# Feed-forward stage of a two-layer decoder trunk: 20 instead of 4 of the 22 inner column tiles computed by rows of tokens, in five blocks of 512, and transposed by transfers

## The chip, the cores and the metric

One Trainium2 chip, one of its cores. The metric is the device time in microseconds (us) of one execution of the whole program; three runs of the kernel before gave 1230.99, 1231.00 and 1232.06 us, so the median is 1231.0 us. A profiled execution lies beside them; every duration in this document that has a row is taken from such a profile.

## What is computed

The input is 256 tokens of 1024 numbers in float32. Two layers each apply a feed-forward half step, a token mixer, and a second feed-forward half step, each followed by a layer norm. Four feed-forward stages in all; the change touches only these. Cut to what matters:

```python
D_MODEL = 1024; SEQ = 256; DEPTH = 2; D_FF = 2816

def _swiglu(x, w1, w3, w2):
    return (jax.nn.silu(x @ w1) * (x @ w3)) @ w2

for l in range(DEPTH):
    h = _swiglu(x, ffn_w1[l, 0], ffn_w3[l, 0], ffn_w2[l, 0])
    x = _layernorm(ALPHA * x + 0.5 * h, ln_g[l, 0], ln_b[l, 0])
    h = _mixer(x, ...)
    x = _layernorm(ALPHA * x + h, ln_g[l, 1], ln_b[l, 1])
    h = _swiglu(x, ffn_w1[l, 1], ffn_w3[l, 1], ffn_w2[l, 1])
    x = _layernorm(ALPHA * x + 0.5 * h, ln_g[l, 2], ln_b[l, 2])
```

The inner width of 2816 is 22 column tiles of 128. All products are float32 products made of three: every operand is split into a high part (`hi`, the value rounded to the format that TensorE multiplies) and the rest (`lo`), and a product is hi·hi + lo·hi + hi·lo.

## The kernel before

**Weights.** `stream` (L148) loads 1 MB of weights (128 x 2048 floats) on SyncE's queue (SP) into one of four `raw` buffers and splits it in two pieces of 1024 columns: ScalarE (ACT) copies each piece into a `hi` buffer (L167), and VectorE (DVE) subtracts to get the `lo` buffer (L169). There are eight `hi` and eight `lo` buffers, used in turn, so a piece can only be split when TensorE (PE) has done with the piece eight before it.

**The stage by columns** (`gemm_a2`, L232). For two column tiles j of the inner width, w1 and w3 of both tiles are streamed (2 MB). The weight piece stands in the array and the tokens move: for each of the four weight tiles 8 matmuls of 512 columns (the hi and the lo part of the 256 tokens beside each other, L242) and 8 of 256 columns with the lo weights (L249). The result has the inner columns on the partitions and the tokens in the row, which is the form that the product with w2 wants as its standing operand. ACT copies half of each bank out (L250), DVE adds (L252), ACT applies Silu (L547), DVE multiplies (L548), and `split` (L195, L196) leaves the tile in `hhi` and `hlo`.

**The stage by rows** (`gemm_b2`, L291, and `gemm_first`, L316, for the very first one). For a block of 512 inner columns, four column tiles, the tokens stand in the array (128 at a time) and the weights move: for each of the two halves of the tokens, each of the two matrices and each of the 8 k-tiles, three matmuls of 512 columns (`three`, L227 to L230). That is 96 matmuls a block, in 16 steps of 6 (`rows_b`, L261); the eight weight pieces are all held from the first half of the tokens, which reads each once, to the second half, which reads each once more and then frees it. After each half of the tokens its result (128 tokens x 512 columns) has the tokens on the partitions and must be transposed. `front` (L521) applies Silu (L524) and multiplies (L525); `turned` (L528) calls `transposed` (L173): GpSimd (POOL) copies the two 16-bit halves of the floats apart (two copies, L184), two 16-bit transposing transfers on SP's queue turn them (L188), POOL puts the halves together again (two copies, L192), and ACT and DVE split the result into `hhi` (L536) and `hlo` (L538).

**Order of the work.** A feed-forward stage before is: one block by rows (column tiles 0 to 3), then nine calls of `gemm_a2` for tiles 4 to 21, then the product with w2 in two passes of 512 output columns, each with 22 k-tiles in 11 steps of 12 matmuls per pass; the first pass keeps the last four k-tiles back to the end of the pass (`tail=4`). The order on PE is the order of the code. On the other engines a scheduler sets it, from data and from `behind`, which puts an instruction after a given one. Small pieces of work run beside PE's as generators: `beside(task, delay)`, `beat(w)` and `yield w` count the progress of PE's work in beats, and a task goes on when its beat has come. ACT, DVE, POOL and SP each work their queue strictly in this order, so an instruction that waits holds back all behind it on its engine.

**Other places that the change touches.** `setup` (L372) loads the tokens and small constants on POOL's queue during the first stage. `bc_load` (L402) loads a norm's gain and bias on POOL's queue into the two `bc` buffers; `Norm.turned` (L479) applies them to the tokens 8 beats after the norm. The `planes` tiles (transposition buffers) come from two `val` buffers.

Of the kernel before, what the change touches and what calls it, by code (L numbers as in the profile page):

```python
# [11 lines left out]
F32 = mybir.dt.float32  # L12
# [4 lines left out]
AF = mybir.ActivationFunctionType  # L17
ALU = mybir.AluOpType
AX = mybir.AxisListType

P = 128
D = 1024
# [3 lines left out]
DEPTH = 2  # L26
DFF = 2816
FT = DFF // P
FB = 4
HEADS = 8  # L30
HD = 64
GROUPS = 8
# [2 lines left out]
CH = 2048  # L35
# [16 lines left out]
def trunk(ctx, tc, x, xT, w13a, w13b, w2, wb, wqk, wa, wbr, wo, gateb, sgug, sgub, sguwT, sgubias, lam, diffg,  # L52
          lng, lnb, lngT, lnbT, cosT, sinT, out):
    nc = tc.nc
    V, A, G, PE = nc.vector, nc.scalar, nc.gpsimd, nc.tensor
# [7 lines left out]
    act = ctx.enter_context(tc.tile_pool(name="act", bufs=27))  # L63
    res = ctx.enter_context(tc.tile_pool(name="res", bufs=2))
# [6 lines left out]
    def name(s):  # L71
        serial[0] += 1
        return f"{s}_{serial[0]}"
# [21 lines left out]
    def t512(s, n=2):  # L95
        return tmp.tile([P, 512], F32, tag="main", name=name(s), bufs=n)
# [37 lines left out]
    def beside(task, delay):  # L134
        tasks.append([clock[0] + delay, task])
# [37 lines left out]
    def transposed(src, out, via, first, second):  # L173

        def planes(v):
            return v.bitcast(U16).rearrange("p (w c) -> p w c", w=2)

        def numbers(v):  # L180
            return v.bitcast(U16).rearrange("p (c w) -> p w c", w=2)

        for w in range(2):
            G.tensor_copy(out=planes(out)[:, w], in_=numbers(src)[:, w])  # L184
        yield first
        with behind(loaded[0]):
            for w in range(2):
                nc.sync.dma_start(planes(via)[:, w].rearrange("p (k t) -> p k t", k=4), planes(out)[:, w],  # L188
                                  transpose=True)
        yield second  # L190
        for w in range(2):
            G.tensor_copy(out=numbers(out)[:, w], in_=planes(via)[:, w])  # L192
# [98 lines left out]
    def gemm_b2(srcs, xh, xl, done, norm=None):  # L291

        lent, after = [()] * 4, [(None, None)] * 4
        if norm:
            lent = [(0, 1), (0,), (), ()]
            after[1:3] = (None, norm.ends[0]), (norm.ends[0], norm.ends[0])
        ps = [[bank() for _ in range(2)] for _ in range(NT)]
        got = [[None] * 4 for _ in range(2)]  # L300
        for t in range(NT):
            for c in range(2):
                if norm:
                    norm.ready(t, c)
                    after[3] = [norm.xlo.get((0, 1))] * 2
                for m in range(2):
                    n = 2 * c + m
                    if t == 0:
                        got[m][2 * c : 2 * c + 2] = stream(srcs[m][:, c * CH : (c + 1) * CH], sub=512, lent=lent[n],
                                                           after=after[n])  # L310
                    for i in range(2 * c, 2 * c + 2):
                        rows_b(ps[t][m], t, 2 * i, got[m][i], xh, xl, KT)
            with behind(latest[0] if t == 0 else None):
                done(t, ps[t])
# [40 lines left out]
    b = side_bank()  # L355
# [159 lines left out]
    def ffn(l, f, i, norm, last=False):  # L515
        xh, xl = parts(both)
        h_hi = [act.tile([P, 512], F32R, tag="slot", name=name("hhi")) for _ in range(FT // 2)]
        h_lo = [act.tile([P, 512], F32R, tag="slot", name=name("hlo")) for _ in range(FT // 2)]
        hh, hl = view(h_hi), view(h_lo)

        def front(t, ps):  # L521
            p = act.tile([P, 2, 512], F32, tag="val", name=name("planes"), bufs=2)
            s = p[:, 1]
            A.activation(s, ps[0], AF.Silu)  # L524
            V.tensor_tensor(out=s, in0=s, in1=ps[1], op=ALU.mult)  # L525
            beside(turned(t, s, p), 0)

        def turned(t, s, p):  # L528
            yield from transposed(s, p[:, 0], p[:, 1], 17, 6)
            x = p[:, 0].rearrange("p (k t) -> p k t", k=4)  # L530
            yield 6
            for j in range(2):
                hi, lo = (v[j].rearrange("p (k t) -> p k t", k=2)[:, :, t * P : (t + 1) * P] for v in (h_hi, h_lo))
                f = x[:, 2 * j : 2 * j + 2]
                with behind(silu[0]):
                    A.activation(hi, f, AF.Copy)  # L536
                with behind(added[0]):
                    V.tensor_tensor(out=lo, in0=f, in1=hi.bitcast(F32), op=ALU.subtract)  # L538

        if norm is None:  # L540
            gemm_first([w13b[l, f, 0], w13b[l, f, 1]], front)
        else:
            gemm_b2([w13b[l, f, 0], w13b[l, f, 1]], xh, xl, front, norm=norm)
        for j in range(FB, FT, 2):
            for m, z in gemm_a2([w13a[l, f, j - FB + m] for m in range(2)], both, lambda m: t512("silu")):
                s = z[:, :T]
                silu[0] = A.activation(s, s, AF.Silu).ins  # L547
                V.tensor_tensor(out=s, in0=s, in1=z[:, T:], op=ALU.mult)  # L548
                split(hh(j + m), hl(j + m), s)
                if norm is None and j + m == FB:  # L550
                    beside(setup(s[:, :1]), 0)
        ln = Norm(l, i, 2.0 * ALPHA, 4.0 * EPS, s[:, :1], last)
        gemm_b(w2[l, f, 0], FT, hh, hl, lambda t, p, c, n: ln.part(t, 0, p))

        def done(t, p, c, n):
            ln.part(t, 512 + c, p)
            if c + n == 512:
                ln.finish(t, ((2, 1.5), (2, 1))[t])

        gemm_b(w2[l, f, 1], FT, hh, hl, done, tail=14, last=((0, 256), (256, 256)) if last else ())  # L560
        return ln.close()
# [228 lines left out]
    norm = None  # L790
# [10 lines left out]
def _layout(i):  # L801
    c = np.ascontiguousarray
    L = DEPTH
    f = {k: np.asarray(v) for k, v in i.items()}
    x = f["x"].reshape(T, D)
    o = {"x": x, "xT": c(x.reshape(T, KT, P).transpose(2, 1, 0)).reshape(P, KT * T)}

    def cols(w):

        k, n = w.shape[-2:]  # L810
        w = w.reshape(*w.shape[:-2], k // P, P, n // P, P)
        a = w.ndim
        return w.transpose(*range(a - 4), a - 2, a - 3, a - 4, a - 1)

    def pairs(w):

        w = cols(w)
        lead = w.shape[:-4]
        n = w.shape[-4]
        w = w.reshape(*lead, n // 2, 2, P, KT, P)  # L820
        a = w.ndim
        return c(w.transpose(*range(a - 4), a - 3, a - 4, a - 2, a - 1)).reshape(*lead, n // 2, P, CH)

    def halves(w):

        k, n = w.shape[-2:]
        w = w.reshape(*w.shape[:-2], k // P, P, n // 512, 512)
        a = w.ndim
        w = c(w.transpose(*range(a - 4), a - 2, a - 3, a - 4, a - 1))
        return w.reshape(*w.shape[:-2], (k // P) * 512)  # L830

    nb = FB * P
    w1, w3 = f["ffn_w1"], f["ffn_w3"]
    o["w13a"] = c(np.stack([cols(w1[..., nb:]), cols(w3[..., nb:])], axis=4)).reshape(L, 2, FT - FB, P, CH)
    o["w13b"] = c(np.concatenate([halves(w1[..., :nb]), halves(w3[..., :nb])], axis=2))
    o["w2"] = halves(f["ffn_w2"])
    u, v, q, k, val, ga, gb = (f["w_in"][:, :, s * D : (s + 1) * D] for s in range(7))
    o["wb"] = np.stack([halves(w) for w in (v, val)], axis=1)
    o["wqk"] = np.stack([pairs(w) for w in (q, k)], axis=2)
    o["wa"] = np.stack([pairs(w) for w in (u, ga, gb)], axis=1)  # L840
    o["wbr"] = pairs(f["w_branch"])
    o["wo"] = halves(f["w_out"])
    o["gateb"] = c(f["gate_b"].reshape(L, 2, KT, P).transpose(3, 0, 1, 2))
    o["sgug"], o["sgub"] = f["sgu_ln_g"], f["sgu_ln_b"]
    o["sguwT"] = c(f["sgu_w"].transpose(0, 3, 1, 2)).reshape(L, P, GROUPS * P)
    o["sgubias"] = f["sgu_b"].reshape(L, GROUPS * P)
    o["lam"] = f["lam"]
# [29 lines left out]
```

## Time and profile before

| What | Value |
|---|---|
| median of three runs | 1231.0 us (1230.99 to 1232.06) |
| the profiled execution | 1231.87 us, its span 1230.2 us (first to last instruction) |
| PE, matmuls | busy 1224.3 us (100% of the span), 6639 matmuls |
| DVE, ACT | busy 890.9 us (72%) and 755.3 us (61%) |
| POOL | busy 161.2 us (13%) |
| DMA | 246.09 MB, mean 200 GB/s |
| granted TensorE clock | 0.999 of full speed |

How to read the views: the page gives for each engine its busy time and share of the span. The chain is the work that ended last, followed back from the last instruction; its pieces in order of time are "start, duration, what, how many". The groups of instructions give for each line, engine and operation the tiles, the count, the busy time and the mean duration of one in ns. Matmuls are pipelined, so the mean duration of one (some 390 ns) is not the distance from one to the next; that distance is read from the chain or from a stretch of the windows. The view of a tile lists the instructions that read or write it with shortest, median and longest duration. A timeline row is "start, duration, engine, line, operation, tiles, count" and in brackets the idle time before and what ended it.

### The profile page before, as it was taken

The page shows a single profiled execution, that of the slowest core. Times are in us where ns is not written, and L with a number is a line of the kernel's source. Part 1 is how long each engine was busy: PE and PEld are TensorE (multiplying, and loading weights), DVE is VectorE, ACT ScalarE, POOL GpSimd, SP SyncE. Part 2 cuts the span into 40 slices and gives each one's busy share as a digit, 9 for nine tenths or more (in the row PEclk, how much of TensorE's full clock was granted, in tenths as well). Part 3 has the DMA queues.
Part 4 walks back from the last instruction along what each step waited for, and adds up shares of the span by engine and source line. Part 5 has one row for each costly group of instructions (what it writes and reads, how often), then busy time and mean ns, then how long its engine had stood idle before and what let it go on. Part 6 is the DMA issues. An engine that isn't in the chain of part 4 may idle for free.

```text
span 1230.2 us, 17916 instructions
## 1 busy us (share of the span) xinstructions
PE 1224.3 (100%) x6639; PEld 1057.5 (86%) x6639; DVE 890.9 (72%) x1532; ACT 755.3 (61%) x1388; POOL 161.2 (13%) x248
## 2 busy tenths in 40 slices
PE   9999999999999999999999999999999999999998
PEld 8888888888888888888888888888888888888887
DVE  6767567886787977665677665678867879766753
ACT  7676446678765566664466664466886654766640
POOL 1300000246400021000021000002462000210000
PEclk9999999999999999999999999999999999999999
DMA  9955645655854747547547547556567456566540
GB/s 344 307 205 181 231 171 176 236 176 167 280 201 140 253 151 230 186 170 256 195 156 225 191 160 254 204 180 205 169 193 277 143 185 226 196 198 205 170 173 35
DMA packets 58089, 246.09 MB, mean 200 GB/s; under 512 B 22752, under 2 KB 23824, under 8 KB 31888
## 3 DMA queue, kind: packets, MB, share of 16 engines
q1 hardware_dynamic: 54032, 232.28, 54.7%
q0 software_dynamic: 3536, 12.13, 3.2%
q8 instruction: 52, 0.85, 0.3%
q10 hardware_dynamic: 432, 0.52, 0.2%
q14 instruction: 37, 0.30, 0.1%
HBM read 235.47 MB, written 1.05 MB: 192 GB/s over the span
## 4 chain that ended last, share of the span: by engine, by line
PE 99%; DMA 0%; DVE 0%; ACT 0%; issue 0%; ACTq 0%
PE bank L242 38%; PE bank L230 36%; PE bank L249 20%; PE bank L345 2%; PE sbank L612 1%; PE sbank L496 1%; PE sbank L664 1%; PE sbank L747 1%; PE sbank L662 0%; DMA xraw<-in_xT 0%; PE sbank L649 0%; PE sbank L654 0%; PE sbank L468 0%; DVE xtok L476 0%; ACT whi L195 0%; DVE st L441 0%
## 5 line engine op out<-in xcount | busy, mean ns | idle before, releaser
L169 DVE TENSOR_TENSOR wlo<-raw,whi 128x1024 fp32r<-128x1024 f32 (+1 forms) x442 | 500.4, 1151 | 225.8 <-PE bank L249 118.5
L167 ACT ACTIVATE whi<-raw 128x1024 fp32r<-128x1024 f32 (+1 forms) x442 | 425.2, 979 | 270.0 <-PE bank L230 132.6
L242 PE MATMUL bank<-x,whi 128*128 128x512 f32 x1792 | 422.7, 391 | 0.0
L242 PEld LDWEIGHTS bank<-x,whi 128*128 128x128 f32 x1792 | 331.5, 188 | 66.7
L249 PE MATMUL bank<-x,wlo 128*128 128x256 f32 x1792 | 231.0, 284 | 0.0
L249 PEld LDWEIGHTS bank<-x,wlo 128*128 128x128 f32 x1792 | 225.6, 191 | 5.6
L230 PE MATMUL bank<-whi,hhi 128*128 128x512 f32 (+1 forms) x374 | 141.2, 378 | 0.0
L230 PE MATMUL bank<-wlo,hhi 128*128 128x512 f32 (+1 forms) x374 | 141.0, 377 | 0.0
L230 PE MATMUL bank<-whi,hlo 128*128 128x512 f32 (+1 forms) x374 | 140.9, 377 | 0.0
L250 ACT ACTIVATE r<-bank 128x256 f32<-128x256 f32 x256 | 96.5, 380 | 67.0 <-PE bank L249 66.8
L230 PE MATMUL bank<-whi,x 128*128 128x512 f32 x328 | 105.7, 393 | 0.0
L230 PEld LDWEIGHTS bank<-whi,hlo 128*128 128x128 f32 x374 | 70.4, 188 | 13.0
L230 PEld LDWEIGHTS bank<-wlo,hhi 128*128 128x128 f32 x374 | 70.4, 188 | 12.7
L230 PEld LDWEIGHTS bank<-whi,hhi 128*128 128x128 f32 x374 | 70.4, 188 | 12.7
L230 PEld LDWEIGHTS bank<-whi,x 128*128 128x128 f32 x328 | 61.6, 188 | 12.6
L230 PE MATMUL bank<-wlo,x 128*128 128x512 f32 x164 | 63.9, 390 | 0.0
L405 POOL DMA_DIRECT2D bc<-in_lng x6 | 3.2, 536 | 454.9 <-DVE bc L404 454.9
L588 POOL TENSOR_TENSOR swap<-swap,sin_t 128x512 f32<-128x512 f32 x16 | 26.5, 1655 | 243.2 <-DMA swap<-z 133.3
L502 ACT ACTIVATE xf<-sbank,ln_b,ln_g 128x128 f32<-128x128 f32 x80 | 30.1, 456 | 40.1 <-PE sbank L496 40.1
L252 DVE TENSOR_TENSOR silu<-bank,r 128x256 f32<-128x256 f32 x144 | 54.2, 417 | 0.0
L184 POOL COPY planes<-planes 128x512 uint16<-128x512 uint16 x16 | 26.1, 1659 | 178.9 <-DVE planes L525 178.9
L437 DVE SCALAR_TENSOR_TENSOR xtok<-xtok,bank 128x512 f32<-128x512 f32 (+1 forms) x25 | 16.5, 662 | 42.2 <-PE bank L230 42.2
(183 smaller groups left out, 1324.1 us busy)
## 6 DMA issues: line engine op xcount, KB each, us to landing
raw<-in_w13a SPq DMA_DIRECT2D x72, 1024.0 KB, 5.0
raw<-in_w SPq DMA_DIRECT2D x40, 1024.0 KB, 4.9
raw<-in_wa SPq DMA_DIRECT2D x24, 1024.0 KB, 6.0
raw<-in_wb SPq DMA_DIRECT2D x16, 1024.0 KB, 5.0
raw<-in_wqk SPq DMA_DIRECT2D x16, 1024.0 KB, 5.1
raw<-in_wbr SPq DMA_DIRECT2D x16, 1024.0 KB, 5.2
raw<-in_w13b SPq DMA_DIRECT2D x12, 1024.0 KB, 4.9
raw<-in_wo SPq DMA_DIRECT2D x8, 1024.0 KB, 4.9
```

The source lines that it names most:

```text
L167: A.activation(h, r, AF.Copy)
L169: V.tensor_tensor(out=w, in0=r, in1=h.bitcast(F32), op=ALU.subtract)
L184: G.tensor_copy(out=planes(out)[:, w], in_=numbers(src)[:, w])
L230: PE.matmul(ps, xx, w, start=start and n == 0, stop=stop and n == 2)
L242: PE.matmul(b[-1], hi[:, k * P : (k + 1) * P], xc(k), start=k == 0, stop=False)
L249: PE.matmul(b[n][:, :T], lo[:, k * P : (k + 1) * P], xc(k)[:, :T], start=False, stop=k == KT - 1)
L250: emptied[0] = A.activation(r[:, s], b[n][:, T:], AF.Copy, scale=scale).ins
L252: a = V.tensor_tensor(out=z[:, s], in0=b[n][:, :T], in1=r[:, s], op=ALU.add)
L345: PE.matmul(ps[t][m], x[:, j, o + t * P : o + (t + 1) * P], y, start=k0 + j == 0 and o == 0 and y is hi, stop=k0 + j == KT - 1 and y is lo)
L437: V.scalar_tensor_tensor(out=self.y[t][:, s], in0=self.y[t][:, s], scalar=self.scale, in1=ps, op0=ALU.mult, op1=ALU.add)
L502: A.activation(xf[:, s], b[:, s], AF.Identity, scale=self.gT[:, f], bias=self.bT[:, f])
L588: turned_by[0] = G.tensor_tensor(out=s3, in0=s3, in1=s, op=ALU.mult).ins
```

## The change

Of each feed-forward stage, column tiles 0 to 15 and 18 to 21 are now computed by rows, in five blocks of 512; only tiles 16 and 17 are left to one call of `gemm_a2`, which stands after the fifth block. The fifth block is tiles 18 to 21, the last four k-tiles of the product with w2. The weights are laid out accordingly (`w13a`, `w13b`). `front` and `turned` take the number of the block; the waits ahead of the transfers become 13.3 and 10.3 beats, and those behind them 0.6. The transposition buffers come from `val` for even blocks and from the norm's `bc` buffers for odd ones. Silu and multiplication of a block are now what `behind(silu[0])` and `behind(added[0])` refer to, and `setup` is called after the first half of the tokens of block 1. Since two lines are new near the top, line numbers are two higher up to `ffn` (the matmul of L230 stands on L232) and five to eleven higher behind it.

```diff
-FB = 4
+NB = 5
+FB = 4 * NB
+FA = FB - 4
...
-        def front(t, ps):
-            p = act.tile([P, 2, 512], F32, tag="val", name=name("planes"), bufs=2)
-            s = p[:, 1]
-            A.activation(s, ps[0], AF.Silu)
-            V.tensor_tensor(out=s, in0=s, in1=ps[1], op=ALU.mult)
-            beside(turned(t, s, p), 0)
-
-        def turned(t, s, p):
-            yield from transposed(s, p[:, 0], p[:, 1], 17, 6)
+        def front(n, wait):
+
+            def done(t, ps):
+                pool, tag = ((act, "val"), (res, "bc"))[n % 2]
+                p = pool.tile([P, D], F32, tag=tag, name=name("planes"), bufs=2).rearrange("p (w c) -> p w c", w=2)
+                s = p[:, 1]
+                silu[0] = A.activation(s, ps[0], AF.Silu).ins
+                added[0] = V.tensor_tensor(out=s, in0=s, in1=ps[1], op=ALU.mult).ins
+                beside(turned(n, t, s, p, wait[t]), 0)
+                if norm is None and (n, t) == (1, 0):
+                    beside(setup(s[:, :1]), 0)
+            return done
+
+        def turned(n, t, s, p, wait):
+            yield from transposed(s, p[:, 0], p[:, 1], wait, 0.6)
             x = p[:, 0].rearrange("p (k t) -> p k t", k=4)
-            yield 6
+            yield 0.6
             for j in range(2):
-                hi, lo = (v[j].rearrange("p (k t) -> p k t", k=2)[:, :, t * P : (t + 1) * P] for v in (h_hi, h_lo))
+                k = (n * 4 if n < NB - 1 else FT - 4) // 2 + j
+                hi, lo = (v[k].rearrange("p (k t) -> p k t", k=2)[:, :, t * P : (t + 1) * P] for v in (h_hi, h_lo))
...
-        if norm is None:
-            gemm_first([w13b[l, f, 0], w13b[l, f, 1]], front)
-        else:
-            gemm_b2([w13b[l, f, 0], w13b[l, f, 1]], xh, xl, front, norm=norm)
-        for j in range(FB, FT, 2):
-            for m, z in gemm_a2([w13a[l, f, j - FB + m] for m in range(2)], both, lambda m: t512("silu")):
+        for n in range(NB):
+            srcs = [w13b[l, f, m * NB + n] for m in range(2)]
+            if n == 0 and norm is None:
+                gemm_first(srcs, front(n, (10.3, 10.3)))
+            else:
+                gemm_b2(srcs, xh, xl, front(n, (13.3, 10.3)), norm=norm if n == 0 else None)
+        for j in range(FA, FT - 4, 2):
+            for m, z in gemm_a2([w13a[l, f, j - FA + m] for m in range(2)], both, lambda m: t512("silu")):
                 s = z[:, :T]
                 silu[0] = A.activation(s, s, AF.Silu).ins
                 V.tensor_tensor(out=s, in0=s, in1=z[:, T:], op=ALU.mult)
                 split(hh(j + m), hl(j + m), s)
-                if norm is None and j + m == FB:
-                    beside(setup(s[:, :1]), 0)
```

How the instructions move, at three places of the first stage. On PE, just after the first block (`bank` is an accumulator bank, `x_129` and `x_130` the two halves of the k-tiles of the tokens, `whi` and `wlo` weight pieces), before:

```order
L242 MATMUL bank_403<-x_129,whi_395 128x512 x4
L242 MATMUL bank_403<-x_130,whi_395 128x512 x4
L242 MATMUL bank_412<-x_129,whi_399 128x512 x4
L242 MATMUL bank_412<-x_130,whi_399 128x512 x4
L249 MATMUL bank_373<-x_129,wlo_366 128x256 x4
L249 MATMUL bank_373<-x_130,wlo_366 128x256 x4
```

and now, in block 1:

```order
L232 MATMUL bank_364<-whi_397,x_129 128x512
L232 MATMUL bank_364<-wlo_398,x_129 128x512
L232 MATMUL bank_364<-whi_397,x_129 128x512 x2
L232 MATMUL bank_364<-wlo_398,x_129 128x512
L232 MATMUL bank_364<-whi_397,x_129 128x512
L232 MATMUL bank_364<-whi_403,x_129 128x512
```

The matmuls of 256 columns are gone there; every one streams 512.

On SP's queue, where the transfers of block 0 stand among the weight loads (`planes_343` is the first half of the tokens of block 0, `planes_360` the second), before:

```order
L154 DMA raw_713<-in_w13a 128x2048
L154 DMA raw_741<-in_w13a 128x2048
L154 DMA raw_834<-in_w13a 128x2048
L188 DMA_TRANSPOSE planes_343<-planes_343 128x4x128 x2
L154 DMA raw_864<-in_w13a 128x2048
L188 DMA_TRANSPOSE planes_360<-planes_360 128x4x128 x2
L154 DMA raw_946<-in_w13a 128x2048
```

and now (`raw_557` to `raw_643` are the four streams of block 2, `raw_739` to `raw_838` those of block 3, `planes_473` and `planes_550` are block 1):

```order
L156 DMA raw_557<-in_w13b 128x2048
L156 DMA raw_585<-in_w13b 128x2048
L190 DMA_TRANSPOSE planes_343<-planes_343 128x4x128 x2
L156 DMA raw_613<-in_w13b 128x2048
L190 DMA_TRANSPOSE planes_360<-planes_360 128x4x128 x2
L156 DMA raw_643<-in_w13b 128x2048
L156 DMA raw_739<-in_w13b 128x2048
L156 DMA raw_780<-in_w13b 128x2048
L190 DMA_TRANSPOSE planes_473<-planes_473 128x4x128 x2
L156 DMA raw_808<-in_w13b 128x2048
L190 DMA_TRANSPOSE planes_550<-planes_550 128x4x128 x2
L156 DMA raw_838<-in_w13b 128x2048
```

So each block's two pairs of transfers now stand before the third and the fourth weight load of the block two later.

On POOL, at the end of the loads of `setup`, before:

```order
L382 DMA ln_b<-in_lnbT 128x48
L382 DMA lam_464<-in_lam 128x512
L192 COPY planes_343<-planes_343 128x512 x2
L192 COPY planes_360<-planes_360 128x512 x2
L405 DMA bc_1392<-in_lng 128x1024
```

and now (`planes_675` is block 2):

```order
L384 DMA ln_b<-in_lnbT 128x48
L384 DMA lam_489<-in_lam 128x512
L194 COPY planes_343<-planes_343 128x512
L194 COPY planes_360<-planes_360 128x512 x2
L186 COPY planes_550<-planes_550 128x512 x2
L194 COPY planes_473<-planes_473 128x512 x2
L194 COPY planes_550<-planes_550 128x512 x2
L186 COPY planes_675<-planes_675 128x512 x2
```

The copies of each later block come behind those of the block before, and the last copy of block 0's first half comes behind the loads.

More of the change, by code (lines that the diff above doesn't have):

```diff
@@ L830, in halves @@
         return w.reshape(*w.shape[:-2], (k // P) * 512)
[L832 to L835, printed above, removed]
+    w13 = f["ffn_w1"], f["ffn_w3"]
+    a, b = FA * P, (FT - 4) * P
+    o["w13a"] = c(np.stack([cols(w[..., a:b]) for w in w13], axis=4)).reshape(L, 2, FT - FB, P, CH)
+    o["w13b"] = c(np.concatenate([halves(np.concatenate([w[..., :a], w[..., b:]], axis=-1)) for w in w13], axis=2))
     o["w2"] = halves(f["ffn_w2"])
```

## The prediction

> **What bounds the kernel now.** I read the page first, then the chain, then windows of two stretches. The busy times and the chain:
>
> ```profile
> PE 1224.3 (100%) x6639; PEld 1057.5 (86%) x6639; DVE 890.9 (72%) x1532; ACT 755.3 (61%) x1388; POOL 161.2 (13%) x248
> PE 99%; DMA 0%; DVE 0%; ACT 0%; issue 0%; ACTq 0%
> ```
>
> TensorE (PE) is 99% of the chain, in a span of 1230.2 us, so only work taken from PE, or a wait put ahead of it, can move the end. Two facts are needed: what PE takes for four column tiles in each of the two ways. Pieces of the chain in order of time (start, us, what; L242 and L249 are the way by columns, L230 the way by rows):
>
> ```profile
> 38.92 7.28 PE bank L242 x32
> 46.20 3.83 PE bank L249 x32
> 50.03 7.28 PE bank L242 x32
> ...
> 127.83 57.15 PE bank L230 x252
> ...
> 315.35 21.79 PE bank L230 x96
> ...
> 440.75 12.25 PE bank L230 x54
> ```
>
> The windows of one call by columns, and of one product of 96 matmuls by rows (the mixer's w_out; us, then busy us and counts of PE, PEld, DVE, ACT, POOL, then clock, DMA share, GB/s):
>
> ```profile
> 38.92:50.03 11.11, 11.11 (x65) 9.84 (x65) 8.10 (x22) 8.08 (x14) 4.97 (x9) 1.00 0.96 266
> 315.35:337.14 21.79, 21.79 (x97) 18.02 (x97) 15.26 (x24) 13.64 (x20) 6.06 (x9) 1.00 0.91 286
> ```
>
> A call for two column tiles starts at 38.92 and the next at 50.03: 11.11 us, 32 x 0.2275 + 32 x 0.1197. Ninety-six matmuls by rows take 21.79 us, 0.2270 each. Both are at the full granted clock, without a gap.
>
> **PE: the term that carries the forecast.** Four column tiles by columns are two calls, 128 matmuls: 2 x 11.11 = 22.22 us. By rows they are 96 matmuls of 512 columns: 21.79 us. Both stream the same columns (64 x 512 + 64 x 256 = 96 x 512); the halves of 256 cost more than half of 227.5 ns, 119.7 - 113.8 = 6 ns each, and 64 of them are the 0.4 us. So a block gains 22.22 - 21.79 = 0.43 us. Each stage turns four blocks, the program 16: **-6.9 us**. Other pieces of the same kind bound it: 54 matmuls in 12.25 us are 0.2269, 252 in 57.15 are 0.2268, and the dearest of the chain
>
> ```profile
> 199.16 12.30 PE bank L230 x54
> ```
>
> is 0.2278 each. A block at 0.2278 is 21.87 us and would leave 16 x 0.35 = -5.6 us; at 0.2268 it is 21.77 and gives -7.2. I take the piece of 96 matmuls, a whole block: -6.9.
>
> **DVE and ACT: relieved, on average.** The groups of instructions, and the view of the transposition tiles (shortest/median/longest ns), with which a block is added up:
>
> ```profile
> L169 DVE TENSOR_TENSOR wlo<-raw,whi 128x512 fp32r<-128x512 f32 x82 | 53.2, 685 | 10.3 <-issue 7.9 <-PE bank L249 2.4
> L167 ACT ACTIVATE whi<-raw 128x512 fp32r<-128x512 f32 x82 | 47.6, 625 | 53.7 <-PE bank L230 43.9 <-PE bank L242 9.5
> L184 POOL COPY planes<-planes 128x512 uint16<-128x512 uint16 x16 | 26.1, 1659 | 178.9 <-DVE planes L525 178.9
> L192 POOL COPY planes<-planes 128x512 uint16<-128x512 uint16 x16 | 16.7, 1087 | 51.4 <-DMA planes<-planes 51.4
> ...
> L184 POOL COPY planes<-planes x16: 607/1574/4887, 26.0 to 1065.2; 128x512 uint16<-128x512 uint16 x16
> L188 SPq DMA_TRANSPOSE planes<-planes x16: 1200/1256/4647, 39.7 to 1079.4; - x16
> L192 POOL COPY planes<-planes x16: 771/908/1749, 51.7 to 1087.6; 128x512 uint16<-128x512 uint16 x16
> L536 ACT ACTIVATE hhi<-planes x16: 398/402/408, 106.8 to 1141.2; 128x256 fp32r<-128x256 f32 x16
> L538 DVE TENSOR_TENSOR hlo<-planes,hhi x16: 415/418/420, 107.4 to 1141.7; 128x256 fp32r<-128x256 f32 x16
> L524 ACT ACTIVATE planes<-bank x8: 583/599/602, 24.5 to 1059.2; 128x512 f32<-128x512 f32 x8
> L525 DVE TENSOR_TENSOR planes<-planes,bank x8: 672/678/687, 25.2 to 1062.9; 128x512 f32<-128x512 f32 x8
> ...
> DMA to landing us min/median/max: 4.8/6.5/12.2
> ```
>
> A block needs of DVE 16 x 0.685 + 2 x 0.678 + 4 x 0.418 = 14.0 us, of ACT 16 x 0.625 + 2 x 0.60 + 4 x 0.40 = 12.8, of POOL 4 x 1.66 + 4 x 1.09 = 11.0, each of 21.79. None is full; since PE is 99% of the chain now, it gains nothing from their lighter load. What may hurt is their order. The eight weight pieces are held until the second half of the tokens, 10.9 us, frees them one each 1.36 us; DVE then splits the next block's at 2 x 0.685 = 1.37 each, the same pace, and the first use of piece i is 10.9 us after the use that freed its buffer, less one step. Of these about 9.5 us, a split takes 2; 7 are spare. In DVE's queue the multiplication after a block's end (L525, 0.68, behind a Silu of 0.60) stands ahead of the last three or four half pieces: ready 1.3 + 4 x 0.69 = 4.0 us after the block's end, used from 8.2 us on. Hidden, with 4 us to spare; without that cover each block would lose what is late. In the three stages behind a norm the loads come close (a SP row, and when ACT could use the load):
>
> ```profile
> 450.82 9.70 SPq L154 DMA_DIRECT2D raw<-in_w13a  x4
> 455.90 2.01 ACT L167 ACTIVATE whi<-raw 128x1024 fp32r<-128x1024 f32 x2 [1.80 <-DMA raw<-in_w13a]
> ```
>
> That load, the first after a raw buffer came free at 450.8, is the fifth after block 0: four were there already, and four are just what block 1 needs from 453 on. The fifth is block 2's, used 21.8 us later. Cost nothing.
>
> **POOL and the transfers: hidden, by sums of waits.** After a block's end come 1.3 us of Silu and multiplication, two copies apart (3.3), the issue of two transfers (2.5, 1.256 each), landing 6.5, two copies together (2.2): ready after 15.8 us, 21.5 with the longest landing of 12.2. The first instructions of ACT and DVE that wait for it stand behind the next block's end, 21.8 us on. The transfers now stand ahead of the fourth load of the block two later; that load leaves SP 7.1 us after the block's end instead of when its raw buffer is free, lands some 6.5 later, and is used 21.8 + 8.2 us after it: 14 spare. At a stage's end the fifth block's tiles are ready 15.8 + 2.2 (the earlier half's copies, ahead on POOL) + 1.6 = 20 us after its end; PE has 11.11 us of the last columns and nine steps of 12 matmuls, 9 x 2.72 = 24.5, before it, 35.6. The norm's gain and bias load behind these copies, and are read only after the product with w2. In the first stage POOL has the loads of `setup` between:
>
> ```profile
> 40.32 1.28 POOL L382 DMA_DIRECT2D xtok<-in_x  x2 [7.35 <-DVE gbh L381]
> ...
> 48.25 0.54 POOL L382 DMA_DIRECT2D lam<-in_lam  x1 [3.49 <-DMA xtok<-in_x]
> ```
>
> They take 8.5 us with a wait inside. Block 1's first half ends at 27.7 + 10.9 = 38.6; with the multiplication, its two copies and the loads the last copy of block 0's first half is done at 38.6 + 1.3 + 3.3 + 8.5 + 1.1 = 52.8. ACT waits for it ahead of splitting the last piece of block 2 (0.4 + 1.25, then DVE 0.7: 55.2), which PE wants at 27.7 + 21.8 + 9.5 = 59.0. Spare 3.8: nothing.
>
> **A rule against this change.** More copies on POOL run beside DVE. The trace shows that they take time from each other: a row of DVE with copies beside it, the copies, and DVE later without them.
>
> ```profile
> 447.61 5.45 DVE L169 TENSOR_TENSOR wlo<-raw,whi 128x1024 fp32r<-128x1024 f32 x4
> ...
> 446.62 3.09 POOL L184 COPY planes<-planes 128x512 uint16<-128x512 uint16 x2 [32.58 <-DVE planes L525]
> ...
> 465.92 2.35 DVE L169 TENSOR_TENSOR wlo<-raw,whi 128x1024 fp32r<-128x1024 f32 x2
> ```
>
> Four subtractions took 5.45 us instead of 4.70: 0.75 for the 2.1 us of copying that lay beside them (447.61 to 449.71), so some 1.1 for a whole pair of 3.09. Four pairs add 4.4 to DVE's 14.0: 18.4 of 21.79. The Trainium skill, "SBUF — State Buffer", section "SBUF: two separate sides", says that GpSimd and a VectorE instruction with two SBUF inputs share a port pair as an exclusive lock: the loser waits for the whole instruction. By that rule the times of both add. If the lock is held only for the shortest copies, the trace has 0.607 and 0.771: 14.0 + 4 x 0.607 + 4 x 0.771 = 19.5, still below 21.79; the slowdown and the copies' spread from 607 to 4887 ns agree with a lock, DVE's loss of 0.75 in 2.1 us says that most of a copy's time beside DVE is its own waiting.
>
> **Sum.** -6.9 on PE, nothing else on the path. The profiled execution's 1231.87 would become 1225.0; it lies 0.9 above the median of 1231.0, so the forecast is 1231.0 - 6.9 = **1224.1 us**, 0.56% less. A measurement of this kernel can tell about 0.2% (2.5 us) from no change.
>
> **Rivals.** (a) Slower: DVE becomes the bound of a block. Place: the splits of the weights beside POOL's copies. If the lock is held for the copies' mean times, a block needs 14.0 + 4 x 1.66 + 4 x 1.09 = 25.0 us in place of the 22.22 of two calls: 16 x 2.8 = +45, **1276 us**. It decides once a pair of copies takes more than (21.79 - 14.0) / 4 = 1.95 us from DVE; the pair above took some 1.1. Chance 0.07. (b) The gain is eaten at the edges: each new block waits some 0.3 us, because a last piece is split late (the 4 us spare gone through a Silu or a copy out of turn); 16 x 0.3 = 4.8, **1228.9 us**, no change to be told. Against it: the mixer's 96 matmuls by the same routine ran without a gap. Chance 0.08. (c) Only the first stage waits, 3 us, if the loads of `setup` take 7 us longer: **1227 us**. For it: the DMA is fullest there. Chance 0.05.
>
> **The numbers.** The forecast has 0.80 (faster); (c) is faster too: 0.85. (b) is the same, 0.08. (a) is slower, 0.07. The forecast's own bounds are 1231.0 - 7.2 and - 5.6, with one microsecond for the spread of runs (1230.99 to 1232.06): 1222.8 to 1226.4. The range reaches to (c) and (b) and leaves out (a): **1222.8 to 1229.0**.
>
> **What would show it.** Right: four PE pieces of 21.8 us a stage in the chain, L249 down from 1792 matmuls with x to 768, PE still 99%, POOL's busy share about twice, no wait of PE for DVE or ACT. The copies of L184 (then L186) stay near 1.6 us and the splits of 512 columns under 0.8. Wrong: gaps on PE after a block's end released by `wlo` (a, b), or one gap near 59 us (c); a block of 96 matmuls over 22.2 us without a gap would break the main term.

## The result, and the profile after

The changed kernel takes **1224.49 us** (median of four runs, 1224.14 to 1224.64), the kernel before 1231.35 us beside it on the same chip (1230.99 to 1232.06). The ratio is 0.9943, with a 95% interval of 0.9926 to 0.9960: 6.9 us less (4.9 to 9.1 by that interval), faster. 1224.1 was forecast.

The busy times and the chain by engine, from the page of the kernel after (PEld is the loading of the standing operand into PE's array, which runs beside the matmuls):

```profile
PE 1216.0 (99%) x6127; PEld 1030.1 (84%) x6127; DVE 884.9 (72%) x1500; ACT 710.8 (58%) x1356; POOL 271.8 (22%) x376
...
PE 99%; DMA 0%; DVE 0%; ACT 0%; issue 0%; ACTq 0%
```

PE is still the whole chain. It has 512 matmuls fewer (16 blocks x 32) and 8.3 us less busy time; the span fell from 1230.2 to 1222.4 us. The chain in order of time (start, us, what): the blocks of the first stage and the call by columns behind them; the mixer's product of 96 matmuls, behind matmuls of 256 columns (L251); and of the second stage the rest of block 0 (54 matmuls) with the four other blocks (384):

```profile
5.42 22.06 PE bank L347 x96
27.48 87.04 PE bank L232 x384
114.52 7.25 PE bank L244 x32
...
311.20 1.91 PE bank L251 x16
313.12 21.79 PE bank L232 x96
...
438.53 99.33 PE bank L232 x438
```

The four later blocks are one piece without a gap, in the first stage and in the second. Block by block (us, then busy us and counts of PE, PEld, DVE, ACT, POOL, then clock, DMA share, GB/s):

```profile
27.48:49.24 21.76, 21.76 (x97) 18.02 (x97) 17.50 (x31) 13.69 (x26) 11.17 (x18) 1.00 0.92 327
49.24:71.00 21.76, 21.76 (x97) 18.02 (x97) 16.54 (x26) 11.31 (x23) 7.07 (x8) 1.00 0.89 240
71.00:92.76 21.76, 21.76 (x97) 18.02 (x97) 14.87 (x31) 14.09 (x26) 5.61 (x8) 1.00 0.80 229
92.76:114.52 21.76, 21.76 (x97) 18.02 (x97) 13.98 (x16) 10.86 (x16) 6.77 (x8) 1.00 0.68 209
```

A block takes 21.76 us where two calls by columns took 22.22: 0.46 less, 16 times, is 7.4 us. The first block of all ended 0.35 us earlier than before (27.48 in place of 5.31 + 22.52 = 27.83); together 7.7 of the 7.8 us by which the spans differ. The 0.35 is hardly the change's doing: in e1_narrow, whose first block is the same as here, that block ended at 27.68. DVE is busy for 15.7 us of a block on average, the most in block 1, where the constants of `setup` come too.

The groups of instructions whose price the argument used:

```profile
L171 DVE TENSOR_TENSOR wlo<-raw,whi 128x512 fp32r<-128x512 f32 x338 | 233.8, 745 | 24.0 <-ACT whi L169 12.0 <-issue 7.9 <-PE bank L251 2.4
L251 PE MATMUL bank<-x,wlo 128*128 128x256 f32 x768 | 103.1, 285 | 0.0
L186 POOL COPY planes<-planes 128x512 uint16<-128x512 uint16 x80 | 85.6, 1096 | 309.0 <-DVE planes L530 309.0
L194 POOL COPY planes<-planes 128x512 uint16<-128x512 uint16 x80 | 66.6, 878 | 106.8 <-DMA planes<-planes 106.3
```

The copies apart take 1.10 us in the mean, not the 1.66 of the few before; the splits of 512 columns 745 ns, not 685. In the view of the transposition tiles (shortest/median/longest ns) half of the copies apart take 943 ns or less, and the transfers land sooner as well (median 6.5 us before):

```profile
L186 POOL COPY planes<-planes x80: 607/943/5160, 25.6 to 1147.9; 128x512 uint16<-128x512 uint16 x80
...
DMA to landing us min/median/max: 2.3/4.7/8.3
```

### The profile page after: what moved, and what is told of

The parts are those of the page before. It is cut to its first block, busy times and chain, and to the rows that moved or that the text cites. A ratio compares the mean times of both kernels' runs of the same rounds, so it can differ in the third digit from the quotient of the medians.

```text
span 1222.4 us, 17217 instructions
## 1 busy us (share of the span) xinstructions
PE 1216.0 (99%) x6127; PEld 1030.1 (84%) x6127; DVE 884.9 (72%) x1500; ACT 710.8 (58%) x1356; POOL 271.8 (22%) x376
## 4 chain that ended last, share of the span: by engine, by line
PE 99%; DMA 0%; DVE 0%; ACT 0%; issue 0%; ACTq 0%
PE bank L232 64%; PE bank L244 19%; PE bank L251 10%; PE bank L347 2%; PE sbank L621 1%; PE sbank L498 1%; PE sbank L673 1%; PE sbank L756 1%; DMA xraw<-in_xT 0%; PE sbank L671 0%; PE sbank L658 0%; PE sbank L663 0%; PE sbank L470 0%; DVE xtok L478 0%; ACT whi L197 0%; DVE st L443 0%
## 5 line engine op out<-in xcount | busy, mean ns | idle before, releaser
L171 DVE TENSOR_TENSOR wlo<-raw,whi 128x512 fp32r<-128x512 f32 (+1 forms) x570 | 523.7, 954 | 137.9 <-ACT whi L169 80.9
L169 ACT ACTIVATE whi<-raw 128x512 fp32r<-128x512 f32 (+1 forms) x570 | 434.5, 800 | 252.5 <-PE bank L232 173.7
L232 PE MATMUL bank<-whi,x 128*128 128x512 f32 x1352 | 420.8, 390 | 0.0
L232 PEld LDWEIGHTS bank<-whi,x 128*128 128x128 f32 x1352 | 253.8, 188 | 52.5
L232 PE MATMUL bank<-wlo,x 128*128 128x512 f32 x676 | 263.1, 389 | 0.0
L244 PE MATMUL bank<-x,whi 128*128 128x512 f32 x768 | 184.6, 392 | 0.0
L244 PEld LDWEIGHTS bank<-x,whi 128*128 128x128 f32 x768 | 141.2, 188 | 28.5
L186 POOL COPY planes<-planes 128x512 uint16<-128x512 uint16 x80 | 85.6, 1096 | 309.0 <-DVE planes L530 309.0
L232 PEld LDWEIGHTS bank<-wlo,x 128*128 128x128 f32 x676 | 126.9, 188 | 26.1
L232 PE MATMUL bank<-whi,hhi 128*128 128x512 f32 (+1 forms) x374 | 141.2, 378 | 0.0
L232 PE MATMUL bank<-wlo,hhi 128*128 128x512 f32 (+1 forms) x374 | 141.0, 377 | 0.0
L232 PE MATMUL bank<-whi,hlo 128*128 128x512 f32 (+1 forms) x374 | 140.9, 377 | 0.0
L251 PE MATMUL bank<-x,wlo 128*128 128x256 f32 x768 | 103.1, 285 | 0.0
L251 PEld LDWEIGHTS bank<-x,wlo 128*128 128x128 f32 x768 | 98.5, 191 | 3.1
L232 PEld LDWEIGHTS bank<-whi,hhi 128*128 128x128 f32 x374 | 70.4, 188 | 12.9
L232 PEld LDWEIGHTS bank<-wlo,hhi 128*128 128x128 f32 x374 | 70.4, 188 | 12.8
L232 PEld LDWEIGHTS bank<-whi,hlo 128*128 128x128 f32 x374 | 70.4, 188 | 12.8
L252 ACT ACTIVATE r<-bank 128x256 f32<-128x256 f32 x128 | 47.5, 376 | 27.4 <-PE bank L251 27.2
```

The lines of the kernel that those rows point to most:

```text
L169: A.activation(h, r, AF.Copy)
L171: V.tensor_tensor(out=w, in0=r, in1=h.bitcast(F32), op=ALU.subtract)
L232: PE.matmul(ps, xx, w, start=start and n == 0, stop=stop and n == 2)
L244: PE.matmul(b[-1], hi[:, k * P : (k + 1) * P], xc(k), start=k == 0, stop=False)
L251: PE.matmul(b[n][:, :T], lo[:, k * P : (k + 1) * P], xc(k)[:, :T], start=False, stop=k == KT - 1)
L252: emptied[0] = A.activation(r[:, s], b[n][:, T:], AF.Copy, scale=scale).ins
```

## The experiments

All start from the changed kernel. Theory: the gain is the narrow matmuls of 256 columns that a block by rows does not have, so it counts blocks, and transposition lies beside PE's work. Rivals: the gain has another source; the transposition costs something that the gain covers; DVE is near its limit beside POOL's copies.

### e1_narrow: narrow matmuls put back into the blocks

In every block but the first of all, the third matmul of a k-tile is cut into two of 256 columns, the last k-tile excepted (`xht`, `xlt`, `wh`, `wl` are the two parts of tokens and weights): 19 blocks x 28 pairs.

```diff
...
+            if narrow and k < kts - 1:
+                PE.matmul(ps[:, :n], xht, wh, start=k == 0, stop=False)
+                PE.matmul(ps[:, :n], xht, wl, start=False, stop=False)
+                for h in (slice(0, T), slice(T, 2 * T)):
+                    PE.matmul(ps[:, h], xlt, wh[:, h], start=False, stop=False)
...
```

> The changed kernel, but in the blocks by rows (all but the very first block of the program) the third matmul of each step, hi weights with lo tokens, is cut into two of 256 columns for seven of the eight k-tiles: 28 matmuls of 512 become 56 of 256 in each of 19 blocks. Same columns streamed, same weights, same transposition, same queues. Theory (the whole gain is that a matmul of 256 columns costs more than half of one of 512): each pair costs 2 x 0.1197 - 0.2270 = 0.0124 us more, 28 x 0.0124 = 0.35 us a block, 19 blocks +6.6 us: 1231.1 us, the gain gone. Rival (the gain comes from relieved DVE and ACT or from waits that went away): the cut changes neither, so 1224.5 us stays.

Measured: 1234.81 us (1233.74 to 1235.26), ratio to the kernel before 1.0021 (1.0012 to 1.0030). The whole gain is gone, and more: 10.3 us over the changed kernel, for 532 pairs, is 19.4 ns a pair where 2 x 119.7 - 227.0 = 12.4 was worked out. The rival, that the width doesn't matter, falls; the price was too low. The timeline of PE inside a block shows the steps (start, us, engine, line; L271 and L272 are the wide ones, L274 the pair):

```profile
475.59 0.40 PE L271 MATMUL bank<-whi,x 128*128 128x512 f32 x1
475.83 0.39 PE L272 MATMUL bank<-wlo,x 128*128 128x512 f32 x1
476.06 0.40 PE L274 MATMUL bank<-whi,x 128*128 128x256 f32 x2
476.29 0.40 PE L271 MATMUL bank<-whi,x 128*128 128x512 f32 x1
...
477.68 0.40 PE L271 MATMUL bank<-whi,x 128*128 128x512 f32 x1
```

Three steps of a k-tile take 477.68 - 475.59 = 2.09 us, 0.697 each, without a gap; three wide ones in the changed kernel are 3 x 0.2267 = 0.680. The pair itself takes no longer than a wide one here; the wide ones beside it have grown. The four later blocks of the first stage show the sum: they end at 116.84, 89.16 us after the first block, which is 22.29 us each in place of 21.76, and 19 x 0.53 is the 10 us.

### e8_grouped: the same narrow matmuls, two pairs together

In each call of `rows_b` the third matmuls of both k-tiles are issued after the four others, so that the width changes 304 times and back in place of 532. The edit is shown against e1_narrow, and cut.

```diff
...
-                for h in (slice(0, T), slice(T, 2 * T)):
-                    PE.matmul(ps[:, h], xlt, wh[:, h], start=False, stop=False)
+                rest.append((k, xlt, wh))
...
+        for k, xlt, wh in rest:
+            for h in (slice(0, T), slice(T, 2 * T)) if k < kts - 1 else (slice(0, 2 * T),):
+                PE.matmul(ps[:, h], xlt, wh[:, h], start=False, stop=k == kts - 1)
```

> As many narrow matmuls as in the kernel that measured 19.4 ns a pair where 2 x 119.7 - 227.0 = 12.4 was expected (532 pairs of 256 columns in place of 532 matmuls of 512), but those of two neighbouring row tiles stand together, so that the width changes from 512 to 256 and back 304 times in place of 532. Theory A (a pair costs 12.4 ns, and each change of width and back 7 ns more): 532 x 12.4 + 304 x 7.0 = 8.7 us over the changed kernel, 1233.2. Theory B (each pair costs 19.4 wherever it stands): 1234.8 again. Theory C (two narrow ones that share the loaded x, as a pair does in either kernel, cost nothing, and the price is that of the first wide one after them, 19.4 ns a change): 304 x 19.4 = 5.9, 1230.4.

Measured: 1236.91 us (1235.70 to 1237.04), ratio 1.0037 (1.0024 to 1.0051): 12.4 us over the changed kernel, 23.3 ns a pair, more than scattered. A, B and C all miss (B by 2.1 us); the price is neither one for each pair nor a fixed one for each change of width. The timeline of PE in a block (L279 are the narrow ones):

```profile
477.13 0.64 PE L279 MATMUL bank<-whi,x 128*128 128x256 f32 x4
477.60 0.40 PE L272 MATMUL bank<-whi,x 128*128 128x512 f32 x1
477.83 0.40 PE L273 MATMUL bank<-wlo,x 128*128 128x512 f32 x1
478.07 0.39 PE L272 MATMUL bank<-whi,x 128*128 128x512 f32 x1
478.30 0.40 PE L273 MATMUL bank<-wlo,x 128*128 128x512 f32 x1
478.53 0.63 PE L279 MATMUL bank<-whi,x 128*128 128x256 f32 x4
```

Four narrow ones take 0.47 us, 117.5 ns each, near the 119.7 of the columns; each of the four wide ones takes 0.2325, all alike, in place of 0.2267. So near narrow matmuls the wide ones slow down too, by some 6 ns, and not only the one that follows.

The traces say how far this reaches. Taken from start to start and averaged over all places of the changed kernel's trace where wide matmuls follow a run of 256 columns, the first five wide ones are 233.0, 235.8, 228.5, 232.4 and 230.9 ns long, and all later ones 226.7. The trace of the kernel before has the same five numbers within 0.2 ns. They add up to 27 ns for each run, the 0.03 us between 7.28 in the kernel before (behind narrow ones) and 7.25 above (behind wide ones). In e1_narrow two wide ones, or five, stand between pairs, in e8_grouped four or five: scattered or grouped, the wide matmuls of a block hardly ever come out of the slow five. What slows these five is open: no wait is in the trace there, and the granted clock is 1.0. Each narrow matmul also has a loading of the standing operand of its own (PEld 6659 times in both kernels, 6127 in the changed one); no run separates this from the width.

### e2_three: three blocks in place of five

```diff
-NB = 5
+NB = 3
```

> Three blocks of 512 by rows in place of five, tiles 8 to 17 by columns: 8 new blocks in the program in place of 16. Theory (0.43 to 0.46 us for each block turned): 1231.35 - 8 x 0.45 = 1227.8 us. Rival (the gain is one of a stage's edge, or mostly of the first block, and does not count blocks): near 1224.5 us, or near 1231.

Measured: 1227.86 us (1227.63 to 1228.42), ratio 0.9969 (0.9956 to 0.9981). Half the turned blocks (8 of 16) give half the gain: without the other eight the time is 1227.86 - 1224.49 = 3.4 us longer, 0.42 each.

### e3_unturned: no transposition

This kernel leaves out the transposition in the feed-forward stages (no copies on POOL, no transposing transfers); ACT and DVE split the untransposed tile in its place.

```diff
-            yield from transposed(s, p[:, 0], p[:, 1], wait, 0.6)
-            x = p[:, 0].rearrange("p (k t) -> p k t", k=4)
+            yield wait
+            yield 0.6
+            x = s.rearrange("p (k t) -> p k t", k=4)
```

> Leaves out the transposition: no copies on POOL and no transposing transfers in the feed-forward stages; the untransposed result is split in their place. All matmuls, splits and loads stay. Theory (the transposition is hidden): 1224.5 us, within 0.5. Rival (it costs something at the edges of the blocks): faster by what it costs, 0.3 us for each of 20 blocks or more, so 1218.5 us or below. DVE's splits of 512 columns show what POOL's copies take from DVE: near 0.685 us each in place of 0.745.

Measured: 1224.76 us (1223.89 to 1224.94), ratio 0.9941 (0.9929 to 0.9954). Without any transposition the time is the same: POOL, the transfers and what they take from DVE lie wholly beside PE. What DVE pays is in its page line and its groups:

```profile
PE 1215.8 (99%) x6127; PEld 1030.0 (84%) x6127; DVE 849.6 (70%) x1500; ACT 710.3 (58%) x1356; POOL 121.5 (10%) x216
...
L171 DVE TENSOR_TENSOR wlo<-raw,whi 128x512 fp32r<-128x512 f32 x338 | 215.6, 686 | 30.7 <-ACT whi L169 17.2 <-issue 7.9 <-PE bank L251 2.4
```

The splits are back at 686 ns, DVE is busy for 849.6 us in place of 884.9: the 160 copies, with the transfers between them, took 35.3 us from it, 0.22 us a copy, 0.44 a pair.

### e4_copies2 and e4_copies4: POOL's copies two and four times over

Each copy of a block's transposition is issued twice, or four times, with the same operands.

```diff
+        times = 2 if first > 10.1 else 1
         for w in range(2):
-            G.tensor_copy(out=planes(out)[:, w], in_=numbers(src)[:, w])
+            for _ in range(times):
+                G.tensor_copy(out=planes(out)[:, w], in_=numbers(src)[:, w])
...
```

> Every copy of GpSimd around a block's transposition is issued twice, with the same result. Measured in the changed kernel, four pairs of copies take 4 x 2 x 1.096 / 2 + 4 x 2 x 0.878 / 2 = 7.9 us of a block of 21.76; twice that is 15.8. Theory (VectorE loses a little beside the copies, and POOL is still short of a block): nothing is late, 1224.5 to 1226.5. Rival (a) of the prediction (VectorE pays the copies' whole time): 14.0 + 15.8 = 29.8 us of VectorE a block, 8 us over, 16 blocks: about 1350 us.

Measured: 1225.50 us (1224.37 to 1226.28), ratio 0.9944 (0.9922 to 0.9966). Doubled copies cost nothing that can be told. The page line:

```profile
PE 1216.5 (99%) x6127; PEld 1030.3 (84%) x6127; DVE 918.3 (75%) x1500; ACT 709.1 (58%) x1356; POOL 426.9 (35%) x536
```

DVE lost another 33.4 us to 160 more copies, 0.21 each; there are no more transfers here, so it is the copies that take the time from DVE.

> Every copy of GpSimd around a block's transposition is issued four times. 4 x 7.9 = 31.6 us of POOL a block of 21.76: POOL itself becomes the bound, the transposed halves fall behind by 9.8 us a block, 49 at a stage's end, of which some 15 are spare there: 34 us a stage, about 1360 us in all, with the gaps at the stages' ends, and blocks of 96 matmuls still near 21.8 us. Rival (VectorE pays the copies' whole time): 14.0 + 31.6 = 45.6 us of VectorE a block, with every block itself stretched to that: over 1600 us. Second rival (the copies repeated on data just read cost little): below 1240 us.

Measured: 1358.27 us (1355.56 to 1361.35), ratio 1.1023 (1.0997 to 1.1049). The time lies within 2 us of the 1360 forecast, in part by luck, as the waits below show. The busy times of the second stage's last blocks and its end show who is full (columns as above):

```profile
541.00:563.00 22.00, 20.97 (x82) 14.43 (x81) 15.66 (x17) 9.20 (x18) 22.00 (x28) 1.00 0.45 147
563.00:585.00 22.00, 20.92 (x85) 15.36 (x85) 15.66 (x17) 8.42 (x13) 22.00 (x26) 1.00 0.48 176
585.00:607.00 22.00, 9.64 (x50) 7.97 (x48) 9.42 (x7) 5.15 (x6) 22.00 (x26) 0.77 0.23 68
607.00:629.00 22.00, 14.11 (x50) 11.41 (x51) 10.19 (x17) 8.13 (x17) 18.85 (x26) 0.69 0.59 202
```

POOL works 22.00 of 22 us, DVE 15.7: the bound is POOL, not DVE. PE waits most at the stage's end, as expected; part of the loss is inside the later blocks, which was not expected (waits of the weight loads of PE, us in total, times, longest; L235 is the blocks and the product with w2, L247 the call by columns):

```profile
PEld bank L235 <- DVE wlo L171: 41.9, 74, 2.7
PEld bank L235 <- DVE silu L257: 41.6, 4, 10.7
...
PEld bank L247 <- DVE planes L533: 38.1, 4, 10.3
```

The waits at the stages' ends make 41.6 + 38.1 = 79.7 us, 20 a stage where 34 were forecast: a block's copies took (272.0 + 296.9) / 20 = 28.4 us of POOL, not 31.6. The 41.9 us of waits in the blocks, and the lower clock behind the stops (0.77 and 0.69 in the last two rows), which the forecast did not have, filled the difference.

### e5_early, e6_early4, e7_earlylast: the waits ahead of the transfers and the copies

`front` holds the transfers back by 13.3 or 10.3 beats. In the first of these kernels both numbers are 0 in all blocks, in the second in the first four of each stage, in the third in the fifth alone.

```diff
-                gemm_first(srcs, front(n, (10.3, 10.3)))
+                gemm_first(srcs, front(n, (0, 0)))
             else:
-                gemm_b2(srcs, xh, xl, front(n, (13.3, 10.3)), norm=norm if n == 0 else None)
+                gemm_b2(srcs, xh, xl, front(n, (0, 0)), norm=norm if n == 0 else None)
```

> The waits in beats ahead of the transfers are 0 in place of 13.3 and 10.3, so that the queues put the transfers and the splits behind them as early as they can: ACT then waits for a block's first transposed half shortly after that block's end, ahead of the last weight pieces of the next block. Theory (spare of some 4 us there, of which the copies and the landing use most): at most 1 us a stage, 1224.5 to 1228 us. Rival (the waits in beats are what hides the transposition, and without them each block loses 1 to 3 us): 1240 us or more.

Measured: 1276.43 us (1275.07 to 1279.40), ratio 1.0368 (1.0353 to 1.0382). My theory, that a transposition with spare time may be issued at any time, is refuted: 51.9 us. What ACT waited for, and PE's weight loads for:

```profile
ACT hhi L545 <- POOL planes L194: 228.6, 40, 11.5
...
PEld bank L232 <- DVE wlo L171: 18.2, 37, 1.7
PEld bank L244 <- ACT planes L529: 11.6, 4, 3.4
PEld bank L232 <- DVE silu L254: 9.2, 4, 3.5
PEld bank L244 <- DVE planes L530: 6.3, 4, 2.3
```

The splits of the transposed tiles (L545) now stand in ACT's queue before their data are there, and hold back what is behind them: the weight splits, and the Silu that empties the banks. In the changed kernel this wait does not occur. I then thought the loss to lie at the stage's end alone, and split it.

> The waits ahead of the transposing transfers and of the second copies are 0 in the first four blocks of a stage and stay as they are in the fifth. Theory (all of the loss seen with no waits at all, 52 us, comes from the fifth block's halves, which then stand in ScalarE's queue ahead of the first column call): 1224.5 to 1228 us. Rival (the loss is shared by the blocks): some four fifths of 52, about 1266 us.

Measured: 1239.75 us (1238.17 to 1241.97), ratio 1.0062 (1.0039 to 1.0084): 15.3 us over the changed kernel. Both expectations miss; the early blocks cost, through late weight pieces (waits of PE's weight loads):

```profile
PEld bank L232 <- DVE wlo L171: 14.9, 32, 1.7
...
PEld bank L244 <- DVE planes L530: 0.5, 1, 0.5
```

> The waits are 0 in the fifth block alone. Theory (the loss sits at the stage's end): about 1276 us, as with no waits at all. Rival (shared by the blocks): about 1235 us.

Measured: 1242.12 us (1241.85 to 1242.70), ratio 1.0080 (1.0062 to 1.0098): 17.6 us. Again both miss. The timeline of ACT at the end of the second stage's call by columns, and the first matmul of the product with w2 on PE (idle time before, and what ended it, in brackets):

```profile
553.20 0.72 ACT L545 ACTIVATE hhi<-planes 128x256 fp32r<-128x256 f32 x2 [4.94 <-POOL planes L194]
553.83 0.91 ACT L252 ACTIVATE r<-bank 128x256 f32<-128x256 f32 x3
...
554.80 0.80 PE L232 MATMUL bank<-whi,hhi 128*128 128x512 f32 x1 [3.81 <-DVE silu L254]
```

The copies out of the banks (L252) stand behind a split that waits 4.94 us for POOL, and PE stands for 3.81. The two parts make 15.3 + 17.6 = 32.9 of the 51.9. The rest appears only where both come together: the call by columns itself waits for the banks of the fifth block, 11.6 + 6.3 = 17.9 us in e5_early, 0.5 in e6_early4, none in e7_earlylast; 50.8 in all. This is an addition of waits and times, not a test of its own: of the 17.9 us by which weight loads came late, the matmuls stood still for 14.1, and stops also lower the clock (last section).

## Why the prediction was right, point by point

**PE, the term that carried it: right, a little too small.** -6.9 forecast, -6.9 by the medians, -7.8 by the spans. A block took 21.76 us, just past the better end of the bounds (21.77 to 21.87), without a gap; the gain counts blocks (e2_three) and goes when narrow matmuls come back (e1_narrow). So the blocks alone give 16 x 0.46 = 7.4 us, and that the medians come to the forecast 6.9 to the tenth is chance, well inside the interval of 4.9 to 9.1. The term missed 0.03 us a block because its sample, the mixer's 96 matmuls, stood behind narrow ones, as it still does (313.12 above, 21.79 us again): it held the five slow wide matmuls, 27 ns, that a block behind a block does not have. Behind the term stood "6 ns each" for the halves of 256. With 119.7 - 226.7 / 2 = 6.35 ns, 64 halves are 0.41 us of the 0.46, and twice 27 ns the other 0.05. This is the price of long runs of one width, which is what the change removed; it is no price for mixing widths, where a pair cost 19 to 23 ns. One reading behind the bounds was wrong and harmless: the piece of 54 in 12.30 us was not the dearest of the chain; 18 matmuls in 4.19 us, from 185.41 on, are 0.233 each, behind matmuls of 128 columns.

**DVE and ACT: right.** DVE 14.0 us a block forecast, 15.7 on average, of 21.76 (with what the copies take, 4 x 0.44, the sum is 15.8); ACT 12.8 and 12.5. The chain has no gap for them in the blocks.

**POOL and the transfers: hidden, as said; two prices were wrong to the safe side.** POOL went from 13% to 22%, less than twice, because the copies of L186 took 1.10 us, not "near 1.6": 12 of the 16 copies before stood behind a norm, where DVE is fullest (3.00 of 3 us from 446 to 458), and were no sample for a whole stage. Landing took 4.7 us in place of 6.5. The timeline of POOL for the fifth block of the second stage, which ends with the piece above at 438.53 + 99.33 = 537.86:

```profile
540.92 2.13 POOL L186 COPY planes<-planes 128x512 uint16<-128x512 uint16 x2
547.13 1.57 POOL L194 COPY planes<-planes 128x512 uint16<-128x512 uint16 x2 [4.08 <-DMA planes<-planes]
```

The copies were done at 548.70, 10.8 us after the block's end where 18.4 were forecast. The last of the splits behind them, which have other work ahead of them on DVE, ended at 559.1, 21.2 us after the block's end: 20 were forecast and 35.6 allowed. That it is hidden is shown by e3_unturned and, with twice the copies, by e4_copies2. The prediction named the cover: "The first instructions of ACT and DVE that wait for it stand behind the next block's end". The last three kernels show that this place in the queue is the cover, more than the spare time: with the same transfers and more time in hand, an earlier place costs up to 52 us.

**The rule against the change, and rival (a): did not come.** A pair of copies took 0.44 us from DVE, not 1.1; the row that gave 1.1 came from one stretch in which DVE had no pause. The Trainium skill, "SBUF — State Buffer", section "SBUF: two separate sides", has the shared port pair as a lock that the first to come keeps for its whole instruction. The trace agrees that both sides lose, DVE 0.22 us a copy, and POOL 0.49 of a copy of L186 (1.10 in the mean, 0.607 at the shortest, if that one is undisturbed); the reading that made it a rival, that DVE pays the whole copy, is refuted by e4_copies2, where it would have cost over 100 us. At four times the copies, an original pair has become four, and these took (996.9 - 849.6) / 80 = 1.84 us from DVE (busy for 996.9 us in e4_copies4), just short of the 1.95 from which the rival decides; but POOL was full first.

**Rivals (b) and (c): did not come.** No gap at a block's end, none near 59 us.

## What to carry to other kernels

Where PE is 99% of the chain, two orders of the same product are compared by the distance between matmuls in stretches without a gap, taken from the chain; 0.5 us a block was enough to forecast 6.9 us, and it pays to take the sample where its neighbours are those of the new order. Here side work beside a full PE was free as long as two things held: its own engine kept up (POOL at twice the copies, not at four times), and each instruction that waits for it stood in its queue behind what PE needs next. The place in the queue has to be checked, not only the time in hand. A busy mean taken from a few instructions in a crowded stretch was too high here (1.66 us against 1.10).

## What the runs showed of the hardware

**A short stop of PE costs more than itself.** In e7_earlylast, after the stop of 3.81 us, the matmuls of 512 columns came every 0.427 us for some 5 us, and the granted clock fell (windows, columns as above):

```profile
126.00:128.00 2.00, 0.58 (x3) 0.49 (x4) 1.73 (x6) 1.96 (x7) 0.00 (x0) 1.00 0.13 53
128.00:130.00 2.00, 2.00 (x10) 1.67 (x9) 2.00 (x7) 1.75 (x6) 0.00 (x0) 1.00 0.03 8
...
550.00:555.00 5.00, 1.19 (x10) 0.99 (x9) 1.35 (x5) 1.76 (x6) 1.42 (x2) 0.86 0.34 105
555.00:560.00 5.00, 5.00 (x12) 3.95 (x13) 5.00 (x13) 2.22 (x7) 0.49 (x1) 0.50 0.17 29
```

After the stop of the first stage, 1.42 us of the two from 126 to 128 and some 0.6 ahead of them, it stayed at 1.00. Twelve matmuls in the place of 22 in those 5 us are some 2.3 us on top of 3.81. In the third stage a shorter stop was enough, the first matmul of the product with w2 again (timeline of PE, same kernel):

```profile
741.73 0.79 PE L232 MATMUL bank<-whi,hhi 128*128 128x512 f32 x1 [2.27 <-DVE silu L254]
742.32 0.63 PE L232 MATMUL bank<-wlo,hhi 128*128 128x512 f32 x1
742.75 0.63 PE L232 MATMUL bank<-whi,hlo 128*128 128x512 f32 x1
...
744.83 0.39 PE L232 MATMUL bank<-wlo,hhi 128*128 128x512 f32 x1
745.06 0.40 PE L232 MATMUL bank<-whi,hlo 128*128 128x512 f32 x1
```

Here the slow matmuls, 0.43 us apart, last for 3 us. In the fourth stage, after a stop of 3.27 us, six matmuls came at the full pace before the distance of 0.427 us began, again for 3 us. The Trainium skill, "TensorE: Matmul & The Clock Gate", section "Part 1: The HAM clock gate (the "warmup" mystery)", gives half the clock after an idle window of about 3.4 us, and the full one after as long a busy one, with windows that run freely. The trace agrees on the half (0.50, and 0.427 against 0.227 us) and roughly on the time back (3 and 5 us); a stop of 2.27 us was enough here, so the stop need not be as long as that window.

**Narrow matmuls slow their neighbours.** A wide matmul took 0.2325 us where narrow ones stood between, 0.2267 where none did, in the same loop, at the same clock; grouping the narrow ones did not help. In four traces (before, after, e1_narrow, e8_grouped) the slow ones are the first five behind a run of 256 columns, or as many as there are, and the sixth takes 0.227 again. The cause is open.
